# Merge gates projected inside the recurrent loop, gate B and the recurrent way out by plain products, in a hybrid attention and RG-LRU layer on one core

## The chip, the cores and the metric

The kernel runs on one core of a Trainium2 chip. The metric is the device time of one execution in microseconds, as the median of several runs. The kernel before took 921.36 us (three runs, 921.23 to 922.41).

The core has a tensor engine (PE; its loading of stationary operands is shown apart as PEld), a vector engine (DVE), a scalar engine (ACT), GpSimd (POOL), and SyncE (SP), whose queue issues the loads of the weights. The program holds one list of instructions for each engine, and semaphores tie the lists together. A tile scheduler makes the lists when the program is built, from the order in which the code records the work.

## The reference, cut to what matters

512 tokens of 1024 features pass through one layer in float32:

```python
xn = rmsnorm(x)
q, k, v, xr, gr, ga, gb = split(xn @ w_in)          # seven blocks of 1024 columns
ya = chunked_band_attention(q, k, v) @ w_attn_out     # 16 heads of 64
xc = causal_depthwise_conv(xr)                        # width 4
yb = (rg_lru(xc) * gelu(gr)) @ w_rnn_out              # gates r, i: block-diagonal products of xc
h = x + (sigmoid(ga + b) * ya + sigmoid(gb + b) * yb) @ w_o
h = h + (silu(g) * up) @ w_ffn_out                    # g, up = split(rmsnorm(h) @ w_ffn_in)
out = rmsnorm_final(h)
```

The change is about `ga` (gate A), `gb` (gate B) and `yb`, the recurrent branch's way out.

## The kernel before, in words

**Operands in two parts.** Every large product is made of three matmuls: an operand is kept as a rounded high part and the exact rest (`split`, L74: ACT copies the high part, DVE subtracts it for the low part), and `mm3` (L68) adds high by high, high by low and low by high. A weight chunk is 1024 rows by 256 columns. `load` (L133) brings it from SP's queue in two halves of 512 KB into a pool of three raw buffers; `prefetch` (L186) splits each half into a tile of 128 by 1024 in a pool of four, so two chunks at a time. `weights(name, ahead)` makes sure that the chunk and `ahead` more are split.

**Plain products.** `project` (L216) makes one tile of 128 outputs by 512 tokens: eight blocks of 128 features, three matmuls each, so 24 matmuls whose moving operand has 512 columns. A chunk of 256 columns is two tiles, 48 matmuls.

**Block products.** `block_product` (L256) makes the same 256 outputs by Winograd's form of Strassen's product: seven products of blocks instead of eight, each of 12 matmuls with 256 moving columns, so 84 matmuls. It pays for that with sums of blocks. `weight_sums` (L154) makes four sums of weight blocks on DVE (128 by 512 each) and splits seven blocks and sums. `block_sums` (L225) makes four sums of the right side on POOL: `xn_tmp`, split into `xn_sum`, for the normed input, and `rnn_t`, split into `rnn_sum`, for the recurrent branch. ACT copies partial results aside (`keep`, L263), DVE adds them up (L276, L277). In the kernel before, six of the eight tiles of gate B and all eight of the recurrent way out are made so; the feed-forward part's `fg` and `fu` as well.

**The stages.** (1) The norm and the first half of `xr0` and `gr0`. (2) The recurrent loop (L550): for each pair of feature tiles, two tiles of `xr` and the convolution (`rnn_conv`, three DVE instructions, then a split with ACT and POOL), two tiles of `gr` and its gelu (`rnn_gelu`), and the RG-LRU gates (`rnn_gates`, L504): small products `rg` in two PSUM buffers of tag "s", tanh and exp on ACT (`gt`, `u`), three DVE instructions and one on POOL (`a`). When both tiles of a pair are that far, a square root, the scan (`rnn_scan`, L527: L528, L529, L530 on DVE) and the split into `rnn`. Between these, POOL makes the sums of the normed input. (3) `q` and `k` of the first two heads, two plain tiles of gate B (`gb0`, `gb1`), then three block products for the rest of gate B, POOL's sums of the recurrent branch, and four block products for its way out (L628 to L670). (4) Attention, head by head (L795), one head's scores ahead of the other's weighing. Between the heads lie plain tiles of later `q`, `k` and `v` (20 tiles' worth over heads 0 to 11, 1.67 a head) and the eight tiles of gate A (two a head, heads 12 to 15). (5) Attention's way out `ya`, the merge, `w_o`, the feed-forward part and the last norm.

## Time and profile before

| | |
|---|---|
| median of three runs | 921.36 us |
| the profiled execution's own time (its span) | 919.8 us |
| PE busy | 880.2 us, 5472 matmuls |
| PEld busy | 789.5 us |
| DVE busy | 631.2 us |
| ACT busy | 503.2 us |
| POOL busy | 212.3 us |
| moved from memory | 86.05 MB read, 97 GB/s in the mean |

The profile gives for the profiled execution the time from its first to its last instruction; the median of the runs is 1.6 us longer. Matmuls are pipelined and their ends are modelled, so neighbouring matmuls overlap in the profile, and a busy PE is not PE at its peak.

### The profile page before, as it was taken

What the parts mean: (1) busy time and instruction counts of PE and PEld (TensorE: products, weight loads), DVE (VectorE), ACT (ScalarE), POOL (GpSimd) and SP (SyncE); (2) the same over time, 40 slices, a digit from 0 to 9 for tenths busy, and PEclk for the clock granted to TensorE, in tenths of its full rate; (3) what the DMA queues carried; (4) which work ended last, traced back from release to release, by engine and by line L of the source; (5) the groups of instructions that cost most, each with busy time, mean ns of one, the idle gap of its engine ahead of it and who ended that gap; (6) DMA issues with size and microseconds to landing.
All of it is one profiled execution on the core that took longest, in us unless ns stands there. A gap on an engine that the chain in (4) does not pass through costs nothing.

```text
span 919.8 us, 14042 instructions
## 1 busy us (share of the span) xinstructions
PE 880.2 (96%) x5472; PEld 789.5 (86%) x5472; DVE 631.2 (69%) x926; ACT 503.2 (55%) x905; POOL 212.3 (23%) x216
## 2 busy tenths in 40 slices
PE   8994989779999999999999999999999999999997
PEld 5983768779989898988888889899999999888886
DVE  5798999999666676665436636899887888463203
ACT  7555678256467685766533436565655555732203
POOL 4579424950023141222100000520000001300200
PEclk9997999889999999999999999999999999999999
DMA  8321321123543232323122703243333332353102
GB/s 255 93 69 46 92 69 46 46 69 116 143 134 91 81 104 81 92 74 99 61 78 92 251 24 92 62 124 119 115 111 104 106 92 93 115 173 125 47 1 92
DMA packets 85026, 89.09 MB, mean 97 GB/s; under 512 B 5344, under 2 KB 73552, under 8 KB 84960
## 3 DMA queue, kind: packets, MB, share of 16 engines
q1 hardware_dynamic: 83584, 84.73, 29.7%
q10 hardware_dynamic: 1376, 3.47, 1.0%
q8 instruction: 43, 0.70, 0.3%
q14 instruction: 23, 0.19, 0.1%
HBM read 86.05 MB, written 2.14 MB: 96 GB/s over the span
## 4 chain that ended last, share of the span: by engine, by line
PE 77%; DVE 13%; ACT 5%; issue 3%; DMA 1%; POOL 1%; SPq 0%; ACTq 0%; DVEq 0%; POOLq 0%
PE po_out L70 4%; PE po_out L72 4%; PE po_out L71 4%; PE o L743 2%; PE p_fu L72 2%; PE p_fu L71 2%; PE p_fu L70 2%; PE p_fg L72 2%; PE p_fg L70 2%; PE p_fg L71 2%; PE pT L723 2%; PE po_v L72 2%; PE po_v L71 2%; PE po_v L70 2%; PE po_ya L70 2%
## 5 line engine op out<-in xcount | busy, mean ns | idle before, releaser
L70 PE MATMUL po_out<-whl_fo,act_hi 128*128 128x512 f32 (+1 forms) x198 | 73.0, 369 | 0.0
L71 PE MATMUL po_out<-whl_fo,act_hi 128*128 128x512 f32 (+1 forms) x198 | 73.0, 369 | 0.0
L72 PE MATMUL po_out<-whl_fo,act_lo 128*128 128x512 f32 (+1 forms) x198 | 72.3, 368 | 0.0
L77 DVE TENSOR_TENSOR whl_fo<-raw_fo,whl_fo 128x1024 fp32r<-128x1024 f32 x22 | 27.9, 1281 | 42.2 <-ACT whl_fo L76 42.2
L943 POOL TENSOR_TENSOR act_lo<-act,act_hi 128x1024 fp32r<-128x1024 f32 x4 | 11.1, 2766 | 181.5 <-ACT act_hi L942 179.7
L76 ACT ACTIVATE whl_fo<-raw_fo 128x1024 fp32r<-128x1024 f32 x22 | 23.0, 1057 | 50.1 <-PE po_out L72 36.6
L711 POOL TENSOR_SCALAR p<-p,rl 128x128 f32<-128x128 f32 (+1 forms) x64 | 34.2, 554 | 66.1 <-DVE rl L709 66.0
L77 DVE TENSOR_TENSOR pp<-pT,pp 128x512 fp32r<-128x512 f32 (+1 forms) x64 | 30.5, 485 | 20.3 <-ACT pp L76 19.9
L72 PEld LDWEIGHTS po_out<-whl_fo,act_lo 128*128 128x128 f32 x198 | 37.2, 188 | 6.8
L70 PEld LDWEIGHTS po_out<-whl_fo,act_hi 128*128 128x128 f32 x198 | 37.2, 188 | 6.7
L71 PEld LDWEIGHTS po_out<-whl_fo,act_hi 128*128 128x128 f32 x198 | 37.2, 188 | 6.6
L708 ACT ACTIVATE p<-p,m 128x128 f32<-128x128 f32 (+3 forms) x64 | 35.5, 556 | 12.0 <-DVE m L707 11.7
L707 DVE CUSTOM_DVE_ANT_0 p<-s,bias 128x128 f32<-128x128 f32 (+3 forms) x64 | 29.9, 485 | 12.5 <-PE s L705 9.3
L72 PE MATMUL po_v<-whl_v,xnT 128*128 128x256 f32 x128 | 36.4, 284 | 0.0
L71 PE MATMUL po_v<-whl_v,xnT 128*128 128x256 f32 x128 | 36.3, 284 | 0.0
L70 PE MATMUL po_v<-whl_v,xnT 128*128 128x256 f32 x128 | 36.3, 283 | 0.0
L743 PE MATMUL o<-pp,v 128*128 128x256 f32 (+2 forms) x128 | 36.0, 337 | 0.0
L76 ACT ACTIVATE pp<-pT 128x512 fp32r<-128x512 f32 (+1 forms) x64 | 26.9, 433 | 12.1 <-PE pT L723 7.9
L905 POOL TENSOR_TENSOR sum_t<-x,x 128x512 f32<-128x512 f32 x2 | 3.6, 1783 | 124.5 <-ACT x L349 124.5
L77 DVE TENSOR_TENSOR whl_fg_s<-s_fg,whl_fg_s 128x1024 fp32r<-128x1024 f32 (+1 forms) x22 | 25.9, 1195 | 4.4 <-ACT whl_fg_s L76 4.4
L71 PE MATMUL po_xr<-xnT,whl_xr 128*128 128x512 f32 (+1 forms) x80 | 28.0, 354 | 0.7 <-DVE xnT L347 0.6
L76 ACT ACTIVATE whl_fg_s<-s_fg 128x1024 fp32r<-128x1024 f32 (+1 forms) x22 | 21.2, 977 | 13.1 <-PE q_fg L72 4.4
(461 smaller groups left out, 3422.3 us busy)
## 6 DMA issues: line engine op xcount, KB each, us to landing
raw_fg<-in_w_ffn_in_dram SPq DMA_DIRECT2D x22, 512.0 KB, 4.6
raw_fu<-in_w_ffn_in_dram SPq DMA_DIRECT2D x22, 512.0 KB, 3.6
raw_fo<-in_w_ffn_out_dram SPq DMA_DIRECT2D x22, 512.0 KB, 4.3
raw_qk<-in_w_in_dram SPq DMA_DIRECT2D x32, 256.0 KB, 3.5
raw_xr<-in_w_in_dram SPq DMA_DIRECT2D x8, 512.0 KB, 5.5
raw_gr<-in_w_in_dram SPq DMA_DIRECT2D x8, 512.0 KB, 3.6
raw_gb<-in_w_in_dram SPq DMA_DIRECT2D x8, 512.0 KB, 3.7
raw_yb<-in_w_rnn_out_dram SPq DMA_DIRECT2D x8, 512.0 KB, 3.5
```

The costliest lines, as they stand in the source:

```text
L70: pe.matmul(o, sh, mh, start=start, stop=False, skip_group_check=parts)
L71: pe.matmul(o, sh, ml, start=False, stop=False, skip_group_check=parts)
L72: pe.matmul(o, sl, mh, start=False, stop=stop, skip_group_check=parts)
L76: act.activation(hi, src, AF.Copy)
L77: dve.tensor_sub(lo, src, f(hi))
L707: dve.tensor_tensor_reduce(prob[qb][:], sc[:, 0:w], bias[:, S - w:S], -1.0, 3e38, ALU.add, ALU.min, nmax[:, qb:qb + 1])
L708: act.activation(prob[qb][:], prob[qb][:], AF.Exp, bias=nmax[:, qb:qb + 1], scale=-1.0, accum_out=lsum[:, qb:qb + 1])
L711: pool.tensor_scalar(prob[qb][:], prob[qb][:], rl[:, qb:qb + 1], 1.0, ALU.mult, ALU.mult)
L723: pe.transpose(pt[:, at * P:(at + 1) * P], prob[qb][:, kb * P:(kb + 1) * P], ident[:])
L743: pe.matmul(po[:, S - n:S], st, pp[i][:, part, lo:lo + n], start=kb == 0 and part == 0, stop=kb == NT - 1 and part == 1)
L905: op(dst[:, 2 * i:2 * i + 2], in0(i), in1(i))
L943: (pool if i in (0, 1, 2, 4) else dve).tensor_sub(lo[:], o[:], f(hi[:]))
```

## The change

Gate A's first four tiles (`ga0`, `ga2`) and all eight tiles of gate B (`gb0` to `gb6`) are now plain tiles inside the recurrent loop, after the `gr` tiles of each pair. The RG-LRU gates of a tile (`gates_of(j)`) are recorded right behind its own `gr` tile; before, they ran one or two tiles behind. The recurrent way out is eight plain tiles, recorded after `v0`, with the first head's scores ahead of its last two tiles. `block_sums`, `xn_sum`, `rnn_t`, `rnn_sum` and the block products of gate B and of the way out are gone; `weight_sums` and `block_product` stay for the feed-forward part. In attention there are 24 tiles to lay between the heads instead of 28, 1.5 a head for all 16. The tiles of the recurrent loop (`rw`) now lie where the norm's tiles lay, and gates A and B have tiles of their own from the start (`z`). The barrier that held loads of weights back at `gb2` is gone. Comments that only vanished are left out here.

```diff
-    rw_stack, rw = opened("rw", 2, "right")
+    z_stack, zp = opened("z", 1, "right")
...
-    strassen = [f"gb{j}" for j in range(2, KT, 2)] + [f"yb{j}" for j in range(0, KT, 2)]
-    strassen += [f"f{w}{j}" for j in range(2, FT, 2) for w in "gu"]
+    strassen = [f"f{w}{j}" for j in range(2, FT, 2) for w in "gu"]
...
         plan(f"xr{j}", cols(w_in, C_XR + j * P))
         plan(f"gr{j}", cols(w_in, C_GR + j * P))
+        if j < 4:
+            plan(f"ga{j}", cols(w_in, C_GA + j * P))
+        plan(f"gb{j}", cols(w_in, C_GB + j * P))
...
-    barrier = ["gb2"]
+    barrier = ["wo1"]
...
+    rw_stack, rw = opened("rw", 2)
...
-    def gates_of(n):
-        while len(conv) > n:
-            held.append(rnn_gates(*conv.pop(0)))
+    def gates_of(j):
+        held.append(rnn_gates(j, *conv.pop(j)))
         if len(held) == 2:
             act.activation(u_pairs[-1][:], u_pairs[-1][:], AF.Sqrt, scale=-1.0)
             while held:
                 rnn.append(rnn_scan(*held.pop(0)))
...
+    def gate(w, j):
+        po = tile_of(f"g{'ab'[w]}{j - j % 2}", j % 2)
+        act.activation((ta, zB)[w][j], po[:], AF.Tanh, bias=hb[:, 16 + 8 * w + j:17 + 8 * w + j], scale=0.5)
+
+    conv = {}
     for j in range(0, KT, 2):
         for c in range(2):
+            conv[j + c] = rnn_conv(j + c, tile_of(f"xr{j}", c, ahead=2))
         for c in range(2):
+            po = tile_of(f"gr{j}", c, "mm" if j == 0 else "t")
+            conv[j + c] += (rnn_gelu(j + c, po),)
+            gates_of(j + c)
+        for w in range(j // 4, 2):
+            for c in range(2):
+                gate(w, j + c)
...
-    for j in range(2, KT, 2):
-        block_product(f"gb{j}", j // 2, xn_right, quarters(zs[j // 2]))
...
-    for j in range(0, KT, 2):
-        y = gs.tile([P, 2, S], F32, tag="y", bufs=1, name=f"yb{j}")
-        block_product(f"yb{j}", j // 2, rnn_right, quarters(y))
-        dve.scalar_tensor_tensor(zs[j // 2][:], tb[j][:], 1.0, y[:], ALU.add, ALU.mult)
...
-    for j in range(KT):
-        steps.append((1.0, lambda j=j: ga_tile(j)))
+    for j in range(4, KT):
+        steps.append((1.0, lambda j=j: gate(0, j)))
...
+    for j in range(KT):
+        if j == 6:
+            prob = scores(0)
+        po = mm_tile(f"po_yb{j}")
+        project(po, weights(f"yb{j - j % 2}"), j % 2, rnn)
+        dve.scalar_tensor_tensor(zB[j], zB[j], 1.0, po[:], ALU.add, ALU.mult)
     for h in range(HEADS):
         pp = transposed(h, prob)
         if h + 1 < HEADS:
             prob = scores(h + 1)
+        fill(1.25 + 1.5 * h)
         weigh(h, pp)
+        fill(2.0 + 1.5 * h)
```

The first place is ACT's order in the recurrent loop, where the first pair's square root and scan results meet the next pair (`rnn0` is the first pair's result, `g2` and `gt2` belong to the second pair's gelu and gates, `xn_sum` is a sum of the normed input). Before:

```order
L546 ACTIVATE u0_634<-u0_634 128x1024
L471 ACTIVATE xn_sum3_1038<-xn_tmp_434 128x1024
L76 ACTIVATE whl_gr4_4_713<-raw_gr4_4_714 128x1024
L534 ACTIVATE rnn0_700<-u0_634 128x512
L498 ACTIVATE g2_743<-po_gr2_718 128x512
L534 ACTIVATE rnn0_700<-u0_634 128x512
L498 ACTIVATE g3_775<-po_gr3_750 128x512
L510 ACT_TABLE_LOAD
L510 ACTIVATE gt2_0_834<-rg2_0_830,hb_380 128x512
```

And now, in the same place (`zb0` is gate B's first tile, `xc2` and `xch2` the second pair's convolution):

```order
L510 ACTIVATE u0_557<-u0_557 128x1024
L76 ACTIVATE whl_gr2_0_749<-raw_gr2_0_750 128x1024
L499 ACTIVATE rnn0_617<-u0_557 128x512
L531 ACT_TABLE_LOAD
L531 ACTIVATE zb0_438<-po_gb0_1_723,hb_380 128x512
L76 ACTIVATE whl_gr2_4_754<-raw_gr2_4_755 128x1024
L499 ACTIVATE rnn0_617<-u0_557 128x512
L452 ACTIVATE xc2_794<-po_xr2_0_769,vc_378 128x512
L76 ACTIVATE whl_ga2_0_759<-raw_ga2_0_760 128x1024
```

The second pair's `gt2` stood behind `rnn0`, with its `rg` products already made; now the second pair's convolution only begins behind `rnn0`, and `gt2` follows six instructions later.

The second place is DVE's order where gate B's third chunk (`gb4`) is made ready. Before, in stage 3, with the sums of blocks (`s21`, `s34`) and four split tiles (`a11`, `s2`, `s3`, `a22`, the last of them later):

```order
L77 TENSOR_TENSOR whl_gb4_a11_1445<-raw_gb4_0_1435,whl_gb4_a11_1445 128x512
L165 TENSOR_TENSOR s21_gb4_1439<-raw_gb4_0_1435,raw_gb4_4_1437 128x512
L168 TENSOR_TENSOR s34_gb4_1440<-raw_gb4_0_1435 128x512
L77 TENSOR_TENSOR whl_gb4_a11_1445<-raw_gb4_4_1437,whl_gb4_a11_1445 128x512
L166 TENSOR_TENSOR s21_gb4_1439<-s21_gb4_1439,raw_gb4_0_1435 128x512
L169 TENSOR_TENSOR s34_gb4_1440<-raw_gb4_4_1437,s21_gb4_1439 128x512
L77 TENSOR_TENSOR whl_gb4_s2_1450<-s21_gb4_1439,whl_gb4_s2_1450 128x2x512
L277 TENSOR_TENSOR zb2_1432<-q_gb2_1460,keepa_gb2_1461 128x512
L77 TENSOR_TENSOR whl_gb4_s3_1453<-s34_gb4_1440,whl_gb4_s3_1453 128x2x512
```

Now, in the recurrent loop, between the convolutions of the third pair (`xc4`, `xc5`):

```order
L454 SCALAR_TENSOR_TENSOR xc4_1115<-po_xr4_0_1090,vc_378,xc4_1115 128x509
L77 TENSOR_TENSOR whl_gb4_0_1080<-raw_gb4_0_1081,whl_gb4_0_1080 128x1024
L77 TENSOR_TENSOR whl_gb4_4_1085<-raw_gb4_4_1086,whl_gb4_4_1085 128x1024
L454 SCALAR_TENSOR_TENSOR xc5_1148<-po_xr4_1_1123,vc_378,xc5_1148 128x511
L454 SCALAR_TENSOR_TENSOR xc5_1148<-po_xr4_1_1123,vc_378,xc5_1148 128x510
L454 SCALAR_TENSOR_TENSOR xc5_1148<-po_xr4_1_1123,vc_378,xc5_1148 128x509
L464 SCALAR_TENSOR_TENSOR g4_1181<-g4_1181,po_gr4_0_1156 128x512
```

The four sums and the additions of partial results are gone from DVE, and the chunk's splits are two instructions that stand among the loop's own.

More of the change, by code (lines that the diff above doesn't have):

```diff
@@ L114, in block_kernel @@
             plan_v(pr // 2)
-    for j in range(0, KT, 2):
+    for j in (4, 6):
         plan(f"ga{j}", cols(w_in, C_GA + j * P))
@@ L161, in weight_sums @@
         sc = room[0]
-        s21, s34 = (pl.tile([P, 2, 4, P], F32, tag=tag, bufs=1, name=f"{tag}_{name}")
-                    for pl, tag in ((tp if name[1] == "b" else sc, "s21"), (sc, "s34")))
+        s21, s34 = (sc.tile([P, 2, 4, P], F32, tag=tag, bufs=1, name=f"{tag}_{name}")
+                    for tag in ("s21", "s34"))
         s2, s1, s3, s4 = s21[:, 0], s21[:, 1], s34[:, 0], s34[:, 1]
@@ L222, in project @@
                 xs[k][:, 0, lo:hi], xs[k][:, 1, lo:hi], k == 0, k == n - 1)
-    def block_sums(eng, blk, t, done):
-        for i, kh, half, less in ((0, 0, 1, (0, 0)), (1, 1, 1, 0), (3, 1, 0, 1), (2, 1, 1, (0, 1))):
-            def terms():
-                yield eng.tensor_sub, blk(kh, half, 0), None if less in (0, 1) else blk(*less, 0)
-                yield eng.tensor_add, None, blk(kh, half, 1)
-                if less not in (0, 1):
-                    yield eng.tensor_sub, None, blk(*less, 1)
-            for op, one, two in terms():
-                n = len(one or two)
-                for m in range(n):
-                    at = slice(4 // n * m, 4 // n * (m + 1))
-                    o = t[i][:, at]
-                    op(o, f(one[m]) if one else o, f(two[m]) if two else t[less][:, at])
-                    yield
-            done(i)
-            yield
     def right_side(blk_at, sums):
@@ L367, in block_kernel @@
     act.copy(gm[:], gm_p[:, 0:8])
[L368 removed]
+    _, xnT = features(xnp, "xn", "xnT")
     def xn_at(k, part, half):
@@ L459, in block_kernel @@
     nm_stack.close()
-    t_stack, tp = opened("sums", 4)
-    xn_sums = [None] * 4
-    xn_tmp = tp.tile([P, 4, 256], F32, tag="tmp", bufs=1, name="xn_tmp")
-    def xn_block(kh, half, part):
-        return [xn_whole[:, k:k + 2, part, half * 256:half * 256 + 256] for k in (4 * kh, 4 * kh + 2)]
-    def xn_sum(i):
-        o = xn_sums[i] = tp.tile([P, 2, 4, 256], F32R, tag="sum", name=f"xn_sum{i}")
-        act.activation(o[:, 0], xn_tmp[:], AF.Copy)
-        for k in (0, 2):
-            pool.tensor_sub(o[:, 1, k:k + 2], xn_tmp[:, k:k + 2], f(o[:, 0, k:k + 2]))
-    xn_steps = block_sums(pool, xn_block, [xn_tmp] * 4, xn_sum)
-    xn_right = right_side(lambda kh, half, part, k: xn_at(4 * kh + k, part, half), xn_sums)
+    rw_stack, rw = opened("rw", 2)
     u_pairs = []
@@ L548, in gates_of, with tile_of @@
                 rnn.append(rnn_scan(*held.pop(0)))
+    def tile_of(name, c, tag="mm", ahead=1):
+        whl = weights(name, ahead)
+        if (name, c) in first:
+            po = first[name, c]
+            project(po, whl, c, xnT, 256, S)
+        else:
+            po = mm_tile(f"po_{name}_{c}", tag)
+            project(po, whl, c, xnT)
+        return po
+    zs = [[zp.tile([P, 2, S], F32, name=f"z{w}{j}") for j in range(0, KT, 2)] for w in "ab"]
+    ta, zB = ([t[j // 2][:, j % 2] for j in range(KT)] for t in zs)
+    def gate(w, j):
+        po = tile_of(f"g{'ab'[w]}{j - j % 2}", j % 2)
+        act.activation((ta, zB)[w][j], po[:], AF.Tanh, bias=hb[:, 16 + 8 * w + j:17 + 8 * w + j], scale=0.5)
+    conv = {}
     for j in range(0, KT, 2):
[L551 removed]
         for c in range(2):
[L553 to L576 removed]
+            conv[j + c] = rnn_conv(j + c, tile_of(f"xr{j}", c, ahead=2))
+        for c in range(2):
+            po = tile_of(f"gr{j}", c, "mm" if j == 0 else "t")
[4 more added lines that the diff above has]
+                gate(w, j + c)
     def blocks(ap):
@@ L779, in block_kernel @@
                 steps.append((0.5, lambda pr=pr, t=t: v_tile(pr // 2, t)))
-    qkv = sum(s[0] for s in steps)
-    for j in range(KT):
-        steps.append((1.0, lambda j=j: ga_tile(j)))
+    for j in range(4, KT):
+        steps.append((1.0, lambda j=j: gate(0, j)))
     spent = 0.0
```

96 lines of the change are left out of this document (3 added, 93 removed).

## The prediction

> **What bounds the kernel now.** I read the page's slices first, then the busy time by stages, then the chain of waits inside the stage that is not full. In the slices each digit is a fortieth of the span, 23 us:
>
> ```profile
> PE   8994989779999999999999999999999999999997
> DVE  5798999999666676665436636899887888463203
> POOL 4579424950023141222100000520000001300200
> PEclk9997999889999999999999999999999999999999
> ```
>
> PE is full nearly everywhere, except in the fourth to ninth slice, where DVE is full and PE's granted clock falls. So the kernel is bound by PE, with one stretch, about 75 to 200 us, that is bound by DVE. That stretch holds the recurrent loop's second half and the block products. How much PE loses there has to be counted in matmuls. The distance between starts, where PE never waits, comes from two pairs of rows of the timeline: 20 steps of 512 columns lie between the first two, 52 steps of 256 columns between the last two.
>
> ```profile
> 483.43 0.40 PE L70 MATMUL po_ya<-aT,whl_ya 128*128 128x512 f32 x1
> 488.12 0.40 PE L72 MATMUL po_ya<-aT,whl_ya 128*128 128x512 f32 x1
> 690.16 0.28 PE L70 MATMUL p_fu<-bt,whl_fu_s 128*128 128x256 f32 x1
> 696.35 0.28 PE L70 MATMUL p_fg<-bt,whl_fg_s 128*128 128x256 f32 x1
> ```
>
> That is 4.69/20 = 0.2345 us for 512 columns and 6.19/52 = 0.119 us for 256. The busy time by stretches (start and end, length, then busy time and count for PE, PEld, DVE, ACT, POOL, granted clock, DMA share, GB/s):
>
> ```profile
> 40.00:75.00 35.00, 35.00 (x155) 28.79 (x154) 33.68 (x42) 19.68 (x26) 26.45 (x19) 1.00 0.23 74
> 75.00:135.00 60.00, 47.16 (x198) 37.70 (x196) 53.97 (x56) 38.34 (x54) 31.20 (x23) 0.91 0.23 70
> 135.00:158.00 23.00, 19.88 (x81) 16.02 (x82) 22.04 (x29) 20.66 (x30) 7.45 (x7) 0.93 0.15 46
> 158.00:200.00 42.00, 30.72 (x205) 29.30 (x205) 41.90 (x29) 16.34 (x29) 38.82 (x22) 0.85 0.20 63
> 200.00:230.00 30.00, 30.00 (x251) 30.00 (x250) 28.07 (x39) 20.47 (x37) 0.00 (x0) 0.99 0.33 106
> 255.00:471.00 216.00, 216.00 (x1259) 190.48 (x1259) 132.60 (x303) 139.43 (x307) 52.36 (x109) 1.00 0.30 88
> ```
>
> From 75 to 158 us the matmuls have 512 columns, from 158 to 200 us 256. Worked at full pace they take 198 x 0.2345 = 46.4, 81 x 0.2345 = 19.0 and 205 x 0.119 = 24.4 us. PE thus loses 13.6 + 4.0 + 17.6 = 35.2 us, and 1.2 us more, because each count holds two matmuls that began before its edge (0.5 + 0.5 + 0.2): **36.4 us**. Before and after that stretch it loses next to nothing (155 x 0.2345 = 36.3 in 35 us; 251 x 0.119 = 29.9 in 30 us).
>
> A rule of the Trainium skill, "Trainium Kernel Development and Optimization", section Performance Expectations, says the same of method: matmul busy time is a bad metric, because matmuls are pipelined. By busy time the same three rows give only 60 - 47.16 + 23 - 19.88 + 42 - 30.72 = 27.2 us, and the forecast below would be 9.2 us longer; 198 matmuls in 60 us against the pace of the starts bear the rule out.
>
> Why PE loses it, in the loop: the longest of its waits, and what ACT and DVE did then (timeline, last bracket: idle time before and its releaser).
>
> ```profile
> PE rg L70 <- ACT gt L510: 16.0, 4, 11.8
> 74.10 1.05 ACT L76 ACTIVATE whl_gr<-raw_gr 128x1024 fp32r<-128x1024 f32 x1
> 83.19 0.63 ACT L534 ACTIVATE rnn<-u 128x512 fp32r<-128x512 f32 x1 [8.04 <-DVE u L530]
> 87.23 0.69 ACT L510 ACTIVATE gt<-rg,hb 128x512 f32<-128x512 f32 x1
> 74.84 4.44 DVE L529 TENSOR_TENSOR_SCAN u<-a,gt 128x512 f32<-128x512 f32 x2
> 81.35 3.42 DVE L530 SCALAR_TENSOR_TENSOR u<-u,g 128x512 f32<-128x512 f32 x2
> 115.40 0.50 PE L70 MATMUL rg<-xch,wrg_r 128*128 128x512 f32 x1 [0.91 <-ACT gt L510]
> ```
>
> `rg` of tile 3 needs the PSUM buffer that `gt` of tile 2 empties; `gt` stands on ACT behind `rnn`, and that waits for DVE, which is slow: 3.42/2 = 1.71 us for one L530. POOL is why, in these rows (groups in 40 to 200 us, then in 200 to 230 us, where POOL did nothing):
>
> ```profile
> L77 DVE TENSOR_TENSOR whl_gb_s<-s_gb,whl_gb_s 128x1024 fp32r<-128x1024 f32 x6 | 12.0, 2002 | 0.0
> L77 DVE TENSOR_TENSOR whl_gr<-raw_gr,whl_gr 128x1024 fp32r<-128x1024 f32 x6 | 11.1, 1852 | 0.0
> L77 DVE TENSOR_TENSOR whl_yb_s<-s_yb,whl_yb_s 128x1024 fp32r<-128x1024 f32 x6 | 7.2, 1217 | 0.4 <-ACT whl_yb_s L76 0.4
> ```
>
> The same split of 128x1024 takes 2.00 us beside a POOL that is 38.82 of 42 us busy, 1.22 us beside an idle one.
>
> **The change, part by part.** *PE's work.* Seven chunks go from 84 matmuls of 256 columns to 48 of 512: 48 x 0.2345 = 11.26 against 84 x 0.119 = 10.00 us, so 1.26 us each and **+8.8 us**. Nothing hides this, since PE sets the pace elsewhere. By the Trainium skill, "TensorE: Matmul & The Clock Gate", section Back-to-back issue gap, a warm matmul takes columns/2.4 ns + 2.5 ns, so 0.2158 and 0.1092 us; an estimate from that page is +1.2 us a chunk and a sum 0.5 us shorter. The rows above are slower (0.2345, 0.119), and I go by them.
>
> *The twelve gate tiles move into the loop.* PE's work there, from `ga0` to the end of `v0`, is 28 tiles of 24 matmuls and 48 small ones for `rg`: (672 + 48) x 0.2345 = 169 us. DVE's work in the same stretch, at the durations it had beside the busy POOL:
>
> ```profile
> L489 DVE SCALAR_TENSOR_TENSOR xc<-po_xr,vc,xc 128x510 f32<-128x510 f32 (+2 forms) x20 | 14.8, 742 | 1.2 <-ACT xc L487 1.1
> L529 DVE TENSOR_TENSOR_SCAN u<-a,gt 128x512 f32<-128x512 f32 x8 | 12.6, 1609 | 0.0
> L523 DVE SCALAR_TENSOR_TENSOR u<-u 128x512 f32<-128x512 f32 x8 | 8.9, 1110 | 0.1
> L530 DVE SCALAR_TENSOR_TENSOR u<-u,g 128x512 f32<-128x512 f32 x8 | 8.7, 1121 | 0.0
> L524 DVE SCALAR_TENSOR_TENSOR gt<-gt,xc 128x512 f32<-128x512 f32 x8 | 8.0, 1004 | 0.4 <-ACT gt L510 0.4
> L519 DVE SCALAR_TENSOR_TENSOR u<-gt,u 128x512 f32<-128x512 f32 x8 | 7.2, 896 | 0.9 <-ACT gt L517 0.9
> L528 DVE SCALAR_TENSOR_TENSOR gt<-gt,u 128x512 f32<-128x512 f32 x8 | 6.5, 853 | 0.6 <-ACT u L546 0.5
> L501 DVE SCALAR_TENSOR_TENSOR g<-g,po_gr 128x512 f32<-128x512 f32 x8 | 5.4, 680 | 3.2 <-ACT g L500 3.1
> ```
>
> A tile costs 3 x 0.742 + 1.609 + 1.110 + 1.121 + 1.004 + 0.896 + 0.853 + 2 x 0.680 (the two gelu steps taken as equal) = 10.2 us, eight tiles 81.5 us. Fourteen chunks (the loop's twelve, `qk0` and `v0`) have 28 splits: 28 x 1.852 = 51.9 us. Together 133 us of 169; at the undisturbed 1.22 us a split it is 116. So even at its worst rate DVE no longer fills the stretch, and PE does. ACT had 38.34 of 60 us there; it loses `xn_sum` and `keep` and gains a tanh a gate tile, and is no bound. The gates' loads move ahead on SP's queue with them: one chunk of 1 MB in 11.26 us is 93 GB/s, against 74 GB/s at a DMA share of 0.23 in 40 to 75 us, where the same slots fed PE without a gap. I cost them at 0. The first head's bias load now stands on SP between `v0` and `yb0` and waits for space that the last `rg` leaves; `yb0` is needed 34 us after that, which is its cover.
>
> *POOL and DVE lose the sums of blocks.* POOL was busy for 26.45 + 31.20 + 7.45 + 38.82 = 103.9 us from 40 to 200 us; what it keeps of that in the loop is three instructions a tile:
>
> ```profile
> L535 POOL TENSOR_TENSOR rnn<-u,rnn 128x512 fp32r<-128x512 f32 x8 | 12.2, 1541 | 12.8 <-ACT rnn L534 12.8
> L492 POOL TENSOR_TENSOR xch<-xc,xch 128x512 fp32r<-128x512 f32 x8 | 12.1, 1517 | 17.5 <-ACT xch L491 10.2 <-issue 7.2
> L521 POOL TENSOR_SCALAR a<-u 128x512 f32<-128x512 f32 x8 | 5.3, 659 | 18.4 <-DVE u L519 18.4
> ```
>
> That is 12.2 + 12.1 + 5.3 = 29.6 us over 169. So DVE should come close to its undisturbed pace. The gain of this part is already in the 36.4 us; I count nothing twice.
>
> *The wait at 76 us.* Now the second pair's convolution only starts behind `rnn0` on ACT, and its `rg` comes two tiles later on PE; the pair's gate tiles (24 x 0.2345 = 5.63 us each; four in the first two pairs, 22.5 us, two in the others, 11.3 us) lie between its last `rg` and the next pair's `xr`, which covers the 8.04 us that ACT waited for. I leave 1.0 us for the whole loop, about the 0.91 us of the second wait; the bounds are 0 and the 11.8 us of the first.
>
> *The way out and attention.* Eight `yb` tiles behind `v0` start six tiles (34 us) after the last `rg`, so `rnn7` is there. Attention loses four tiles of cover, from 1.67 and 2 a head to 1.5; from 255 to 471 us PE was full with DVE at 132.6 and ACT at 139.4 of 216 us, so I cost this at 0; if the cover is gone, see the third rival.
>
> **The sum**, against the profiled execution's span: 919.8 - 36.4 + 8.8 + 1.0 = 893.2 us. The median of the runs before, 921.36, is 1.6 us above its span, so the same again: **894.8 us**, 26.6 us or 2.9% faster.
>
> **Rivals.** *First: the loop keeps its wait.* If ACT still stands behind `rnn0` long enough to starve PE once, the 11.8 us stay instead of 1.0: 894.8 + 10.8 = 905.6 us. For it: ACT's order keeps a square root and both `rnn` ahead of the next convolution. Against it: the gate tiles' cover. There is a rule for it too, worked out here as a mechanism: if each of POOL's remaining instructions blocked DVE for its whole length, DVE would have 116 + 30 = 146 us, still below 169. The Trainium skill states it in "SBUF — State Buffer", section Who interferes with whom: a DVE instruction with two SBUF inputs contends with a GpSimd instruction that reads SBUF; the 2.00 against 1.22 us agree. Chance 0.12 for this rival.
>
> *Second, slower: splits late by one chunk after another.* Each chunk may only be split when the chunk two before has left its slots. If the loop's in-order splits then come late by one slow split, 1.85 us, at each of 18 chunks (14, and four `yb`), PE loses 33.3 us: 894.8 - 1.0 + 33.3 = 927 us. It decides from 27.6/18 = 1.5 us a chunk. Against it: no wait of that kind among PE's waits in 40 to 75 us. Chance 0.03.
>
> *Third: attention is paced by its own chain,* softmax and transposes, and keeps its 216 us though four tiles left it: 4 x 5.63 = 22.5 us are not won, 917.3 us. Against it: PE never waited there. Chance 0.05.
>
> *Fourth: the change doesn't do what it says.* The sums leave DVE, but DVE's list stays the pace, because its instructions wait in order for slots and PSUM, and PE loses the same 36.4 us less the 8.8 us that it now works: 921.4 us, no change. The row of 75 to 135 us is for it (DVE 53.97 of 60 us), the 133 of 169 us against. Chance 0.02.
>
> **How the numbers follow.** The forecast has 0.78. Its own low end: all loop waits gone (-1.0), and the start of the feed-forward part, whose order of tiles shifts, losing nothing any more:
>
> ```profile
> 575.00:598.00 23.00, 21.32 (x163) 20.69 (x161) 20.34 (x23) 13.00 (x24) 13.86 (x8) 0.93 0.21 64
> 598.00:621.00 23.00, 22.28 (x187) 22.08 (x186) 21.05 (x26) 14.57 (x26) 5.93 (x4) 1.00 0.40 121
> ```
>
> There 46 - (163 + 187) x 0.119 = 4.3 us are lost, so 894.8 - 1.0 - 4.3 = 889.5; with 0.5 for the spacing, 889. The high end takes in the first rival: 906. About 0.2% of 921 us is what a measurement of this kernel tells from no change (its three runs lie within 1.2 us). Faster by more: 0.78 + 0.12 + 0.05 = 0.95; same 0.02; slower 0.03.
>
> **What would show it.** Right: PE's slices at 9 from the third on, granted clock 1.00 from 75 to 200 us, about 8.8 us more of PE's matmul work, DVE's 128x1024 splits near 1.2 to 1.4 us in the loop, and the profile's start of attention earlier by about what the span loses less the four tiles. Wrong: a wait of PE for ACT or DVE of several us at the turn from one pair to the next (first rival), small waits for `whl` at every chunk (second), or waits for `pT` or `p` between the heads (third).

## The result and the profile after

The changed kernel took 901.17 us (median of four runs, 899.63 to 901.51) beside 921.88 us of the kernel before on the same chip (four runs, 921.23 to 922.84): a ratio of 0.9774, 95% interval 0.976 to 0.9788, so 2.3% faster. The profiled execution's span is 899.1 us, 20.7 us less than the 919.8 us of before. The forecast was 894.8 us.

The slices of the changed kernel, each 22.5 us:

```profile
PE   8999999999999999999999999899999999999997
DVE  5776556553466676666546455998888887453203
POOL 4012112120023222222100002510000001300100
PEclk9999999999999999999999999899999999999999
```

PE is at 9 from the second slice on, but for the feed-forward part's start and the end, and DVE and POOL are no longer full anywhere in the loop. The stretches of the prediction, in the changed kernel (start and end, length, then busy time and count for PE, PEld, DVE, ACT, POOL, granted clock, DMA share, GB/s):

```profile
75.00:135.00 60.00, 60.00 (x265) 49.42 (x265) 35.33 (x41) 34.35 (x46) 10.03 (x9) 1.00 0.30 90
135.00:158.00 23.00, 23.00 (x103) 19.02 (x102) 15.65 (x18) 14.84 (x20) 5.68 (x4) 1.00 0.30 89
158.00:200.00 42.00, 42.00 (x211) 35.68 (x210) 25.81 (x32) 25.04 (x35) 8.19 (x10) 1.00 0.37 112
255.00:445.00 190.00, 185.09 (x1073) 162.15 (x1073) 119.21 (x271) 121.00 (x274) 50.85 (x101) 0.99 0.28 81
```

The first three rows are full, at a clock of 1.00: 265 matmuls in the 60 us in which the kernel before made 198. The last row is attention, and it is not full any more: PE is idle for 4.9 us, where the kernel before had no idle time in 216 us. PE's waits in the whole execution say the same; in the recurrent loop there is none of note, and the longest stand in attention (`o`, `s`) and at the feed-forward part's start (`q_fg`). A row gives the sum in us, how often, and the longest:

```profile
PE o L659 <- ACT pp L76: 3.0, 2, 1.5
PE q_fg L70 <- ACT whl_fg_s L76: 1.9, 1, 1.9
PE q_fg L72 <- DVE whl_fg_s L77: 1.2, 1, 1.2
PE s L620 <- ACT kh L582: 1.2, 3, 0.8
```

How much each stage won or lost is read from the first starts in the timeline: attention's first transpose `pT`, and the first matmul of its way out, `po_ya`. The kernel before, with the first matmul of the second pair's `q` as well, which lies ahead of `pT` there:

```profile
248.43 0.40 PE L70 MATMUL po_q<-xnT,whl_qk 128*128 128x512 f32 x1
267.17 0.38 PE L723 MATMUL pT<-ident,p 128*128 128x128 f32 x2
471.05 0.39 PE L70 MATMUL po_ya<-aT,whl_ya 128*128 128x512 f32 x1
```

The changed kernel, with two rows of a stretch of `xr` and two of the way out for the distance between starts:

```profile
63.71 0.39 PE L70 MATMUL po_xr<-xnT,whl_xr 128*128 128x512 f32 x1
74.59 0.39 PE L70 MATMUL po_gr<-xnT,whl_gr 128*128 128x512 f32 x1
205.16 0.39 PE L71 MATMUL po_yb<-rnn,whl_yb 128*128 128x512 f32 x1
237.01 0.40 PE L72 MATMUL po_yb<-rnn,whl_yb 128*128 128x512 f32 x1
250.00 0.27 PE L639 MATMUL pT<-ident,p 128*128 128x128 f32 x1
448.81 0.40 PE L70 MATMUL po_ya<-aT,whl_ya 128*128 128x512 f32 x1
```

Forty-eight steps lie between the first two, 10.88/48 = 0.227 us, and 136 between the next two, 31.85/136 = 0.2342 us. Over all tiles that read the normed input the steps are 0.2275 us. So gate B's three chunks, the way out and the block products that they replace come to 144 x 0.2275 + 192 x 0.2342 - 588 x 0.119 = **7.8 us** more work.

*Attention.* It took 471.05 - 267.17 = 203.9 us before and 448.81 - 250.00 = 198.8 us now. Four gate tiles less are 96 x 0.2275 = 21.8 us, and 34 matmuls of the second pair's `q` and `k`, 7.7 us, which before lay ahead of the first `pT`, now lie behind it. So 203.9 - 21.8 + 7.7 = 189.8 us was due, and **9.0 us** are lost. *The stretch ahead of it.* Up to the first `pT` the changed kernel has 21.8 + 7.8 - 7.7 = 21.8 us more to do and is there 17.2 us earlier: PE won back **39.0 us**. *Behind it.* From `po_ya` to the first `po_out` (786.73 us before, 766.03 now) it takes 317.2 instead of 315.7 us, **1.5 us** more. The sum, -39.0 + 7.8 + 9.0 + 1.5 = -20.7 us, is the difference of the two spans. The 39.0, 9.0 and 1.5 us are remainders of one profiled execution of each kernel, so a few tenths of a us in them mean nothing.

The splits on DVE, and the RG-LRU step whose operands all lie in SBUF, from 39 to 200 us of the changed kernel:

```profile
L77 DVE TENSOR_TENSOR whl_gb<-raw_gb,whl_gb 128x1024 fp32r<-128x1024 f32 x8 | 10.6, 1319 | 4.7 <-ACT whl_gb L76 4.7
L77 DVE TENSOR_TENSOR whl_gr<-raw_gr,whl_gr 128x1024 fp32r<-128x1024 f32 x6 | 7.3, 1222 | 6.4 <-ACT whl_gr L76 6.4
L488 DVE SCALAR_TENSOR_TENSOR u<-u 128x512 f32<-128x512 f32 x8 | 5.5, 688 | 5.3 <-POOL a L486 5.3
```

A split takes 1.2 to 1.3 us where it took 1.85 and 2.00, and the step 0.69 us where it took 1.11.

What stands in attention's longest wait is seen on ACT's list (timeline, changed kernel):

```profile
361.37 0.39 ACT L76 ACTIVATE pp<-pT 128x256 fp32r<-128x256 f32 x1 [0.92 <-PE pT L639]
362.53 0.59 ACT L580 ACTIVATE kh<-po_k 64x512 fp32r<-64x512 f32 x1 [0.77 <-PE po_k L72]
363.02 1.04 ACT L76 ACTIVATE whl_v<-raw_v 128x1024 fp32r<-128x1024 f32 x1
363.97 0.71 ACT L624 ACTIVATE p<-p,m 128x512 f32<-128x512 f32 x1
364.67 0.26 ACT L76 ACTIVATE pp<-pT 128x128 fp32r<-128x128 f32 x1
```

PE's last tile before `o`, `po_k`, ends at about 362.5 us. `o` then needs the last piece of `pp`, which stands on ACT behind `kh`, the copy for a chunk of `v`, and an exponential, and is made at 364.9 us. The two waits of this kind come to 3.0 of the 9.0 us, and all idle time of attention to 4.9. The rest is lost in a busy PE whose matmuls start farther apart: the granted clock of 0.93 from 400 to 425 us makes about 1.8 us of it (an estimate, 0.07 x 25); what makes the other 2.3 us was not traced.

### The profile page after: what moved, and what is told of

Same layout as the page of the kernel before. It is cut to its first block, busy times and chain, and to the rows that moved or that the text cites. A ratio compares the mean times of both kernels' runs of the same rounds, so it can differ in the third digit from the quotient of the medians.

```text
span 899.1 us, 13343 instructions
## 1 busy us (share of the span) xinstructions
PE 881.4 (98%) x5220; PEld 778.1 (87%) x5220; DVE 553.6 (62%) x863; ACT 473.5 (53%) x841; POOL 133.1 (15%) x168
## 4 chain that ended last, share of the span: by engine, by line
PE 92%; DVE 3%; ACT 2%; issue 1%; DMA 1%; POOL 1%; SPq 0%; DVEq 0%; ACTq 0%; POOLq 0%
PE po_out L70 5%; PE po_out L72 5%; PE po_out L71 5%; PE p_fu L71 2%; PE p_fu L70 2%; PE p_fu L72 2%; PE p_fg L72 2%; PE p_fg L71 2%; PE p_fg L70 2%; PE o L659 2%; PE po_ga L70 2%; PE pT L639 2%; PE po_ga L71 2%; PE po_ga L72 2%; PE po_ya L70 2%; PE po_ya L71 2%
## 5 line engine op out<-in xcount | busy, mean ns | idle before, releaser
L627 POOL TENSOR_SCALAR p<-p,rl 128x128 f32<-128x128 f32 (+1 forms) x64 | 37.4, 605 | 84.4 <-DVE rl L625 83.8
L623 DVE CUSTOM_DVE_ANT_0 p<-s,bias 128x128 f32<-128x128 f32 (+3 forms) x64 | 29.8, 487 | 22.6 <-PE s L621 21.8
L839 POOL TENSOR_TENSOR act_lo<-act,act_hi 128x1024 fp32r<-128x1024 f32 x4 | 10.5, 2624 | 184.1 <-ACT act_hi L838 182.7
L77 DVE TENSOR_TENSOR pp<-pT,pp 128x256 fp32r<-128x256 f32 (+2 forms) x64 | 30.4, 486 | 10.4 <-ACT pp L76 10.0
L72 PE MATMUL po_v<-whl_v,xnT 128*128 128x256 f32 x128 | 36.4, 284 | 0.0
L76 ACT ACTIVATE pp<-pT 128x256 fp32r<-128x256 f32 (+2 forms) x64 | 26.5, 433 | 10.8 <-DVE pp L77 6.3
L77 DVE TENSOR_TENSOR whl_fu_s<-s_fu,whl_fu_s 128x1024 fp32r<-128x1024 f32 x20 | 25.3, 1280 | 5.7 <-ACT whl_fu_s L76 5.6
L639 PE MATMUL pT<-ident,p 128*128 128x128 f32 x160 | 27.5, 273 | 0.7 <-POOL p L627 0.7
L70 PE MATMUL po_gr<-xnT,whl_gr 128*128 128x512 f32 (+1 forms) x80 | 27.8, 349 | 0.1
```

The source lines that it names most:

```text
L70: pe.matmul(o, sh, mh, start=start, stop=False, skip_group_check=parts)
L72: pe.matmul(o, sl, mh, start=False, stop=stop, skip_group_check=parts)
L76: act.activation(hi, src, AF.Copy)
L77: dve.tensor_sub(lo, src, f(hi))
L623: dve.tensor_tensor_reduce(prob[qb][:], sc[:, 0:w], bias[:, S - w:S], -1.0, 3e38, ALU.add, ALU.min, nmax[:, qb:qb + 1])
L627: pool.tensor_scalar(prob[qb][:], prob[qb][:], rl[:, qb:qb + 1], 1.0, ALU.mult, ALU.mult)
```

## The experiments

Two questions were open: where the 6 us between 894.8 and 901.2 us went, and which part of the change filled the loop. The first four runs belong to the first question, the next five to the second, and the last three follow from both. All ratios are to the kernel before on the same chip; the runs were spread over several chips, and its median was 921.5 to 921.9 us on each.

| run | median, us | ratio, 95% interval |
|---|---|---|
| changed kernel | 901.17 | 0.9774 (0.976 to 0.9788) |
| gate A back in attention | 892.38 | 0.9681 (0.9665 to 0.9698) |
| tiles laid towards the first heads | 895.39 | 0.9717 (0.9702 to 0.9731) |
| all of gate A in the loop | 899.28 | 0.9755 (0.9741 to 0.977) |
| high parts on POOL | 910.41 | 0.9878 (0.9859 to 0.9897) |
| before, POOL's sums left out | 890.18 | 0.9657 (0.9641 to 0.9673) |
| before, gate B plain behind the loop | 901.66 | 0.9786 (0.9772 to 0.9801) |
| changed, two loads a tile on POOL | 944.63 | 1.0249 (1.0234 to 1.0265) |
| changed, one load a tile on POOL | 921.99 | 1.0003 (0.9994 to 1.0013) |
| changed, paced load on POOL | 902.44 | 0.9795 (0.9781 to 0.981) |
| gate A back, counter at 21 | 891.93 | 0.968 (0.9666 to 0.9695) |
| gate B plain, sums on DVE | 890.57 | 0.9665 (0.9649 to 0.9682) |
| the same, gate B's first tiles ahead | 888.07 | 0.9636 (0.9622 to 0.9649) |

### Gate A back in attention

```diff
-        if j < 4:
-            plan(f"ga{j}", cols(w_in, C_GA + j * P))
...
-        for w in range(j // 4, 2):
-            for c in range(2):
-                gate(w, j + c)
+        for c in range(2):
+            gate(1, j + c)
...
-        fill(1.25 + 1.5 * h)
+        fill(1.5 + 1.75 * h)
         weigh(h, pp)
-        fill(2.0 + 1.5 * h)
+        fill(2.25 + 1.75 * h)
```

> The changed kernel with all eight gate A tiles laid between the heads again (28 tiles, 1.75 a head); only gate B stays in the recurrent loop. Theory (attention lacks cover): in the changed kernel attention takes 198.8 us from its first pT to its first po_ya; by the kernel before (203.9 us, plus 34 matmuls of q and k that lay ahead of it there, 7.7 us, less four tiles, 21.8 us) it should take 189.8. The 9.0 us are lost cover, so with 28 tiles they come back: 901.2 - 9.0 = 892 us, with no wait of PE for pp or kh over 0.5 us. Rival (the loop needs the two gate A chunks as cover for the turn of a pair): attention gains 9 us, but the wait at the pair's turn comes back, up to 11.8 us: 892 to 904 us, with a wait of xr or rg in the loop. Rival (the loss is no matter of cover): 901 us.

It took 892.38 us. The loop's stretch from 75 to 135 us, and the starts of attention and of its way out:

```profile
75.00:135.00 60.00, 60.00 (x265) 49.53 (x264) 42.62 (x51) 39.31 (x52) 13.92 (x11) 1.00 0.29 88
```

```profile
228.10 0.27 PE L636 MATMUL pT<-ident,p 128*128 128x128 f32 x1
440.80 0.39 PE L70 MATMUL po_ya<-aT,whl_ya 128*128 128x512 f32 x1
```

The loop stays full with two gate tiles a pair. Attention takes 212.7 us, against 203.9 + 7.7 = 211.6 due. So, as the theory had it, the lost cover was 8 to 9 us, and the two gate A chunks in the loop bought nothing there.

### Tiles laid towards the first heads

```diff
-        fill(1.25 + 1.5 * h)
+        fill(20 * (h + 0.9) / 12 if h < 12 else h + 8.5)
         weigh(h, pp)
-        fill(2.0 + 1.5 * h)
+        fill(20 * (h + 1.3) / 12 if h < 12 else h + 9)
```

> The changed kernel with its 24 tiles laid as in the kernel before: 1.67 a head over heads 0 to 11, then 1 a head for heads 12 to 15 (instead of 1.5 a head throughout). Theory (cover is needed head by head where keys and value chunks are made ready, in heads 0 to 11; the last heads, which make no q, k or v, need less): with no tile at all heads 12 to 15 cost the run before this some 6 us, so with one each at most half of that: 892 to 896 us. Rival (it is the number of tiles in all that counts): 901 us, as the changed kernel.

It took 895.39 us: with the same 24 tiles 5.8 us of the loss are gone. Where the tiles lie counts, not their number alone.

### All of gate A in the loop

```diff
-        for w in range(j // 4, 2):
+        for w in range(2):
...
-        fill(1.25 + 1.5 * h)
+        fill(20 * (h + 0.9) / 12)
         weigh(h, pp)
-        fill(2.0 + 1.5 * h)
+        fill(20 * (h + 1.3) / 12)
```

> The changed kernel with all eight gate A tiles in the recurrent loop; attention has 20 tiles, laid over heads 0 to 11 (1.67 a head, the kernel before's own spacing), and heads 12 to 15 have none. Theory: PE's work is the same; heads 0 to 11 lose at most 1 to 2 us, since at 1.67 a head the kernel before had no idle time; heads 12 to 15 have only their own matmuls, about 3.7 us a head (189.8 us less 24 tiles of 5.46 us, by 16), against a chain of scores, softmax, transposes and splits that the ACT list alone makes 6 to 8 us long: 3 to 5 us lost a head, 12 to 20 us in all; 901.2 - 8 + 12 to 20 = 905 to 913 us. Rival (a head's own chain costs PE nothing, and the loss comes from the loop's end or from the loads): 893 to 901 us.

It took 899.28 us, less than expected. Its stretches in attention, the second with the heads that have no tile:

```profile
350.00:400.00 50.00, 50.00 (x315) 45.16 (x314) 33.08 (x72) 34.34 (x78) 12.68 (x24) 1.00 0.30 90
400.00:450.00 50.00, 46.77 (x277) 39.25 (x276) 36.17 (x94) 36.31 (x90) 16.47 (x36) 1.00 0.22 64
```

Heads 0 to 11 are full at 1.67 tiles a head. Attention takes 174.7 us, against 212.7 - 8 x 5.46 = 169.0 by the run with gate A back (5.46 us is 24 x 0.2275): four heads without any tile cost 5.7 us, not 12 to 20. This fits a short chain in the last heads, which make no `q`, `k` or `v`, and a need of cover in the heads that do; the run before points the same way.

### High parts on POOL

```diff
+                elif name[:2] in ("qk", "ga", "v1", "v2", "v3") and name != "qk0" and index[name] > index["yb6"]:
+                    pool.tensor_copy(hl[:, 0], raw[:])
+                    dve.tensor_sub(hl[:, 1], raw[:], f(hl[:, 0]))
```

> The changed kernel, but POOL instead of ACT makes the high parts of the weight chunks used in attention (22 copies of 128x1024 leave ACT's list, 1.05 us each). Theory (the two long waits come from ACT's list, where such a copy stands ahead of the pp evacuation): the waits for pp at 365 and 413 us shrink from 1.5 us to under 0.5, and attention gains 4 to 9 us: 892 to 897 us. Rival (a head's chain as a whole, DVE and POOL too, is too long for 1.5 tiles): the waits stay or move to POOL's p, which now stands behind the copies: 900 to 906 us.

It took 910.41 us, slower than the changed kernel and outside both ranges. PE's waits:

```profile
PE s L623 <- DVE m L626: 4.6, 4, 1.5
PE o L662 <- ACT pp L76: 2.5, 4, 1.1
PE o L662 <- DVE pp L77: 2.0, 2, 1.8
```

The wait for `pp` by ACT is shorter, but waits for DVE take its place. So ACT's copy at 363 us cannot be called the cause by itself; the chain of such a head as a whole is too long for what lies over it. What each of its steps costs was not separated. The run is no clean test of ACT's list either: beside POOL's copies DVE's splits of `qk` take 1.37 us instead of 1.24.

### Before, POOL's sums left out

```diff
-            for op, one, two in terms():
...
+            if i == 0 or t[i] is not t[0]:
+                eng.memset(t[i][:], 0.0)
...
-        for k in (0, 2):
-            pool.tensor_sub(o[:, 1, k:k + 2], xn_tmp[:, k:k + 2], f(o[:, 0, k:k + 2]))
+        pool.memset(f(o[:, 1]), 0.0)
```

> The kernel before with POOL's sums of blocks left out: xn_tmp and rnn_t are set to zero once and the low parts of xn_sum are zero, so gate B and the recurrent way out are not those of the reference; matmuls, weight sums and ACT's work are unchanged. It tells what POOL's work beside DVE cost. Theory (POOL slows DVE, and DVE holds PE up from 75 to 200 us): the splits of 128x1024 fall from 1.85 and 2.00 us to about 1.25, and of the 38 us that PE lost there at least 26 come back; a wait of rg for gt of up to 11.8 us may stay: 921.9 - 26 to 38 = 884 to 896 us. Rival (DVE's own sums of weights and additions are too much, with POOL or without): at most 13 us come back: 909 us or more.

It took 890.18 us, 31.6 us faster than before, with all of DVE's sums, every block product and the old order. It leaves POOL's sums out of gate B and the way out, with zeros in their place. Two of its stretches, and a group from 39 to 200 us:

```profile
75.00:135.00 60.00, 56.66 (x242) 45.89 (x241) 54.49 (x67) 47.27 (x67) 16.68 (x14) 0.97 0.24 71
158.00:200.00 42.00, 41.28 (x342) 40.81 (x341) 35.99 (x50) 27.81 (x49) 0.00 (x0) 1.00 0.32 101
```

```profile
L77 DVE TENSOR_TENSOR whl_gb_s<-s_gb,whl_gb_s 128x1024 fp32r<-128x1024 f32 x6 | 7.3, 1218 | 0.8 <-ACT whl_gb_s L76 0.8
```

DVE is busy for 54.49 of 60 us, as much as before (53.97), but it gets 67 instructions done instead of 56, and PE 242 matmuls instead of 198. The block products alone, with a quiet POOL, run nearly without a gap from 158 to 200 us: 342 matmuls where before made 205.

### Before, gate B plain behind the loop

```diff
-    strassen = [f"gb{j}" for j in range(2, KT, 2)] + [f"yb{j}" for j in range(0, KT, 2)]
+    strassen = [f"yb{j}" for j in range(0, KT, 2)]
...
-    xn_steps = block_sums(pool, xn_block, [xn_tmp] * 4, xn_sum)
+    xn_steps = iter(())
...
-        block_product(f"gb{j}", j // 2, xn_right, quarters(zs[j // 2]))
...
+            project(pb, weights(f"gb{j}", 1), c, xnT)
```

> The kernel before with one part of the change alone: all of gate B by plain products, where it stood, behind the loop; no sums of the normed x; no tile moves into the loop, and the way out keeps its block products. PE's work grows by three chunks, 48 x 0.2275 - 84 x 0.119 = 0.9 us each, 2.8 us. Theory (the sums are what cost, not the order of the tiles): from 75 to 158 us POOL keeps three instructions a tile, DVE's splits fall to about 1.25 us, and most of the 20 us lost there come back, less a wait of rg of up to 11.8 us; from 158 to 200 us six plain tiles lie over POOL's sums of the recurrent branch, and most of the 18 us come back too: 921.9 + 2.8 - 26 to 38 = 887 to 899 us. Rival (PE needs the gate tiles inside the loop, since the convolution and gates of a pair are a chain that only other tiles cover): the loop keeps 12 us or more of its loss: 899 to 912 us.

Besides, the barrier that held loads of weights back at `gb2` moves to `yb0`. It took 901.66 us, the changed kernel's time, with no tile moved into the loop. Its stretches:

```profile
75.00:135.00 60.00, 58.07 (x247) 47.05 (x246) 53.63 (x65) 48.02 (x66) 16.57 (x15) 0.97 0.24 72
158.00:200.00 42.00, 34.73 (x199) 31.07 (x198) 34.38 (x30) 17.89 (x27) 22.80 (x13) 0.88 0.21 68
```

The loop is almost full without any gate tile in it (247 matmuls, against 265, so 4.1 us less work done), and PE waits there for `gt` for 1.9 us in all instead of 16.0. Most of what is left is lost from 158 to 200 us, beside POOL's sums of the recurrent branch. That part of the expectation, that most of the second loss comes back too, was wrong, and so the time fell into the rival's range, though not for the rival's reason.

### Loads on POOL in the changed kernel

Two loads ahead of each full tile of the loop (one in the second run):

```diff
+        if (name, c) not in first and index[name] <= index["gb6"]:
+            for k in (0, 4):
+                pool.tensor_sub(ptmp[:], f(xn_whole[:, k:k + 2, 0]), f(xn_whole[:, k + 2:k + 4, 0]))
```

> The changed kernel with two useless subtractions of 128x1024 on POOL (two SBUF operands each) ahead of each tile of the loop that has 512 columns throughout: 48 of them, about 3 us each, so that POOL is nearly full there as in the kernel before. It tells whether the loop is full because POOL went quiet, or because it has more PE work for the same DVE work. Theory (the tiles): the splits of 128x1024 on DVE slow down from 1.22 to about 1.9 us and DVE's other SBUF work likewise, to some 133 of 169 us, and PE stays nearly full; POOL's own three instructions a tile queue behind the load and may cost a few waits: 901 to 908 us. Rival (the quiet POOL is what counts): DVE is the pace again, and the loop loses 12 us or more: over 913 us.

> The changed kernel with one useless subtraction of 128x1024 on POOL ahead of each full tile of the loop, 24 of 2.77 us, 66 us, so that POOL is busy for about 96 of 161 us, as it was in the kernel before (103.9 of 160). With two the loop lost 43 us, which spoke against the theory that the tiles alone keep PE full; but POOL was then busy for 152 of 191 us and its own steps stood behind the load. Theory as it stands now (DVE's slowing goes with POOL's busy share, and the tiles give some slack): the splits take 1.7 to 2.0 us, PE loses 5 to 15 us: 906 to 916 us. Rival (the tiles alone suffice at the old load of POOL): 901 to 904 us. Rival (a busy POOL undoes the whole gain): 920 us or more.

The paced load, two subtractions of 128x512 behind each of 24 tiles, the first of which reads what ACT or DVE made of the tile:

```diff
+    def pool_load(made):
+        pool.tensor_sub(ptmp[:], f(xnT[0][:, 0]), made)
+        pool.tensor_sub(ptmp[:], f(xnT[0][:, 0]), f(xnT[1][:, 0]))
```

> The changed kernel with useless subtractions of 128x512 on POOL (two SBUF operands, two behind each of 24 tiles of the loop), but each pair of them waits for what ACT and DVE make of its tile, so that the load is spread over the loop instead of running ahead: 48 x 1.5 = 72 us, with POOL's own 30 us some 100 of 161 us, 0.62, as in the kernel before (103.9 of 160). The run with the unpaced load gave 922 us, but there POOL was 46 of 60 us busy from 75 to 135 us, and xch once waited 6.5 us behind the load. Theory (the gate tiles give PE cover enough at the old load of POOL, 133 us of DVE in 169): 901 to 905 us. Rival (DVE slowed down to the old rate is late at each step, whatever the sum of its work): 908 to 922 us, with waits of PE for whl or xch in the loop.

They took 944.63, 921.99 and 902.44 us: the first two in the range of the rival by which a busy POOL undoes the gain, the third in that of the theory. The stretch from 75 to 135 us, and groups from 75 to 115 us, of the run with one load a tile:

```profile
75.00:135.00 60.00, 48.62 (x192) 38.65 (x191) 51.37 (x36) 26.76 (x36) 46.22 (x22) 0.90 0.22 68
```

```profile
L77 DVE TENSOR_TENSOR whl_gb<-raw_gb,whl_gb 128x1024 fp32r<-128x1024 f32 x2 | 6.3, 3132 | 0.5 <-ACT whl_gb L76 0.5
L488 DVE SCALAR_TENSOR_TENSOR u<-u 128x512 f32<-128x512 f32 x1 | 2.9, 2877 | 2.3 <-POOL a L486 2.3
```

The same two of the paced run:

```profile
75.00:135.00 60.00, 59.76 (x263) 48.98 (x262) 43.87 (x43) 33.60 (x46) 49.84 (x33) 1.00 0.32 97
```

```profile
L77 DVE TENSOR_TENSOR whl_gb<-raw_gb,whl_gb 128x1024 fp32r<-128x1024 f32 x2 | 3.2, 1616 | 0.2 <-ACT whl_gb L76 0.2
L488 DVE SCALAR_TENSOR_TENSOR u<-u 128x512 f32<-128x512 f32 x2 | 3.5, 1769 | 3.7 <-POOL a L486 3.7
```

POOL is busy for about the same time in both, 46.2 and 49.8 of 60 us. Beside instructions of 128x1024 that run ahead, DVE gets 36 instructions done and PE 192 matmuls; beside instructions of half that size that come one after the other with the tiles, 43 and 263. From 40 to 200 us POOL was busy for 111 us in the paced run, more than the 103.9 of before, and PE lost next to nothing; in the run with one load a tile it was busy for only 84 us, nearly all of it before 117 us, and PE lost 20.8. So the prediction's claim holds at a load that is spread, and fails at one that is dense. Two things are at work in the dense runs. POOL's own step `xch` stands behind the load: PE waited 6.5 us for it with one load a tile and 14.7 us with two. And DVE is late: with one load a tile PE waited 2.8 us for `whl_gr`, 2.6 for `g` and 2.4 for `whl_xr`; with two, the splits of `gb` took 2.6 us in the mean. The paced run is not quite the old state either: from 39 to 200 us its splits of `gb` and `gr` took 1.65 and 1.39 us, where the kernel before had 2.00 (`gb_s`) and 1.85. The size of POOL's instructions and their place in its list changed together here; how much of PE's loss each of them makes was not tried apart. What the size does to a single split is in the last section.

The Trainium skill, "SBUF — State Buffer", section Who interferes with whom, calls the port pair that DVE and GpSimd share an exclusive lock, and says of DVE's two-port modes that whoever issues first holds it for the whole instruction and the other is blocked. The splits, which read two SBUF operands, behave so: they are longer beside the longer subtraction (3.13 and 1.62 us, against 1.24 us in the same window of the changed kernel).

### The feed-forward part's start

```diff
-    slots, loads = [0], [0]
+    slots, loads = [21], [0]
```

> The kernel with all of gate A back in attention (892.4 us), and the counter that says which fifth weight tile of the feed-forward block products lies in a place of its own starts at 21, as it stood there in the kernel before. Theory: in the changed kernel the two waits of q_fg at the feed-forward part's start (1.9 and 1.2 us) come from that shift, since the same stretch lost 1.2 us less in the kernel before: 891 us, with those waits changed. Rival (the waits are those of the norm and of the first sums, whatever the place): 892.4 us, within 0.5.

It took 891.93 us, 0.45 us less than without this edit, and the two intervals overlap. The waits changed (`q_fu` 1.7 and `q_fg` 1.6 us instead of 1.9 and 1.2), and their sum hardly. From the first `p_fg` to the first `po_out` it is 200.3 us instead of 200.9, and 200.2 in the kernel before; in the other runs it lies between 200.9 and 202.4 us. The run with POOL's sums left out, whose code behind attention is that of the kernel before, also takes 317.1 us from the first `po_ya` to the first `po_out`, like the changed kernel (317.2) and not like the kernel before (315.7); so the shift of places is not needed for it. Where the 1.5 us behind attention come from stays open.

### Gate B plain, with the recurrent sums on DVE

```diff
-    for _ in block_sums(pool, rnn_block, rnn_t, lambda i: None):
+    for _ in block_sums(dve, rnn_block, rnn_t, lambda i: None):
```

> The run with all of gate B by plain products behind the loop (901.7 us), but the sums of the recurrent branch (18 additions, 33.8 us on POOL there) are made on DVE. Theory (what hurts is POOL beside DVE, not the sums): on DVE alone the 18 take 0.69 us each, 12.4 us, the splits of gb fall from 1.80 to about 1.25 us, and the 8 to 10 us that PE lost from 158 to 200 us (waits for yb's weight tiles, 4.7 us the longest) mostly go: 891 to 896 us. Rival (the sums are too much for DVE there, POOL or not): 900 us or more.

One word more than the run with gate B plain, and 11.1 us: 890.57 us. The stretch that was late there, and the largest of the sums on DVE from 39 to 200 us:

```profile
158.00:200.00 42.00, 42.00 (x297) 39.48 (x296) 35.73 (x48) 23.81 (x40) 0.00 (x0) 1.00 0.33 101
```

```profile
L240 DVE TENSOR_TENSOR rnn_t<-rnn_t,rnn 128x512 f32<-128x512 f32 x12 | 7.7, 678 | 0.0
```

On POOL, in the run with gate B plain, the same twelve took 1854 ns each:

```profile
L240 POOL TENSOR_TENSOR rnn_t<-rnn_t,rnn 128x512 f32<-128x512 f32 x12 | 21.9, 1854 | 0.0
```

DVE takes the sums on and is still in time; the stretch is full, and the way out keeps its block products, which are cheaper for PE. Whether DVE could take gate B's sums as well, so that every block product stays, was not tried.

### The same, with gate B's first two tiles ahead

```diff
+    gb_tile(0, tb[0][:, 0])
     gates_of(1)
-    q_tile(0)
+    gb_tile(1, tb[0][:, 1])
     gates_of(0)
+    q_tile(0)
     k_tile(0)
-    gb_tile(0, tb[0][:, 0])
-    gb_tile(1, tb[0][:, 1])
```

> The run with gate B by plain products behind the loop and the recurrent branch's sums on DVE (890.6 us), with gate B's first two tiles ahead of the last pair's rg products instead of q and k of the first heads, which then come behind them. In that run PE loses about 2.5 us from 114 to 124 us, where rg waits for gt (1.8 us) between q and k. Theory (a few tiles at the one place where the chain is late do what twelve in the loop did): that wait goes, 888 to 889 us. Rival (the chain is late by more than the two tiles cover, 10.9 us, or q and k are then late for the first scores): 890.6 us or more.

The list of chunks follows the new order, which is left out here. It took 888.07 us, as the theory had it, and is the fastest of all, 13.1 us below the changed kernel's median. The loop is full, and PE's wait of `rg` for `gt` is gone:

```profile
75.00:135.00 60.00, 60.00 (x264) 49.27 (x263) 51.24 (x61) 47.60 (x65) 17.02 (x14) 1.00 0.27 84
```

## Why the prediction was right or wrong, by its own steps

| term of the sum | predicted, us | measured, us |
|---|---|---|
| PE's loss from 75 to 200 us, won back | -36.4 | -39.0 |
| waits left in the loop | +1.0 | 0, in the line above |
| more work for PE | +8.8 | +7.8 |
| attention | 0 | +9.0 |
| behind attention | 0 | +1.5 |
| sum of the spans' difference | -26.6 | -20.7 |

*What bounds the kernel* was read rightly, and the count of matmuls by the pace of their starts gave the gain to within 2.6 us. The pace itself was taken from the wrong tile: 0.2345 us is that of `po_ya`; tiles that read the normed input go at 0.2275. That made the loss too small and the extra work too large, and with 0.2275 the same rows give 15.0 + 4.6 + 17.6 + 1.2 = 38.4 us for the loss, near the 39.0 of the starts.

*The step that failed* is this one: "Attention loses four tiles of cover, from 1.67 and 2 a head to 1.5; from 255 to 471 us PE was full with DVE at 132.6 and ACT at 139.4 of 216 us, so I cost this at 0". A mean over 16 heads does not show the head in which `kh`, a chunk's copy, an exponential and `pp` stand in a row. The third rival had the mechanism, with a price of 22.5 us for all four tiles; 9.0 of it came true. Gate A back in attention and the other spacing show it from both sides; which steps of such a head make it too long is only in part shown.

*The range.* The measured 901.2 us lies in the stated 889 to 906, but its upper end stood there for the wait in the loop, which went. That the 10.5 us of attention and behind it fit into that room is luck, and so is it that 4.6 us of them are hidden by the three terms above that came out better than forecast (2.6, 1.0 and 1.0).

*The wait at 76 us* went, as forecast, and none took its place. The reason given, cover by the gate tiles, is not the main one: with gate B plain behind the loop, and no gate tile in it, the wait is down from 16.0 to 1.9 us. Two gate tiles a pair cover what is left.

*That DVE would not fill the stretch* was right for the change, and DVE's splits fell to 1.2 to 1.3 us as expected. Of the reasons given, two turn out to do the same work, either one by itself. A quiet POOL alone wins 31.6 us in the old order; the gate tiles in the loop alone keep PE full beside a POOL that is busy for 111 of 160 us, if its load is spread. The reason put first, "even at its worst rate DVE no longer fills the stretch", leaves out how POOL's work lies: beside a dense load the changed kernel loses 20.8 us, all that the change won, with POOL busy for no more than 46 of 60 us. There the short stretches count, not the sum over 161 us.

*The sign for attention's start*, earlier by what the span loses less the four tiles, gives 26.6 - 22.5 = 4.1 us by the forecast's own numbers; it is 17.2 us. It left out the 7.7 us of `q` and `k` that slipped behind that start; the rest are the three terms that came out better (4.6 us) and the tiles' own price, 21.8 instead of 22.5 us.

The other rivals: no wait of the loop stayed (first), no split was late (second), and DVE's list did not stay the pace (fourth).

## What to carry to other kernels

When tiles are taken out of a stage in which PE never waits, the stage's mean of the other engines says little; look for the longest row of steps that one pass puts on one engine's list, and ask what PE has to do meanwhile. Before trading a cheaper product for a plain one to be rid of its sums, try the sums on the engine that is quicker at them: here one word, which put the sums of the way out on DVE, was worth 11.1 us with the cheaper products kept. And cost an engine that slows another by where its load lies and how long its single instructions are, not by its share of the stage.
